# A recurrent chain's last step: the kept-back weight split is issued behind the copies of UV instead of behind the state update

## The chip, the cores and the metric

The kernel runs on one core of one Trainium2 chip. The metric is the device time of one execution in microseconds (us), lower is better; the time of a kernel is the median of several runs. Engines are named as in the profile: PE is TensorE's matmul, PEld its weight load, DVE is VectorE, ACT is ScalarE, POOL is GpSimd, and SP is the queue that issues nearly all DMAs.

## What is computed

One inference step of a hybrid streaming layer over 512 prompt positions and 64 sample positions (576 columns) with model width 2048: an RMSNorm, one input projection to 10880 columns, an RWKV-7 branch (16 heads of 64, a recurrent matrix state), a sliding-window attention branch, two output projections gated and merged, a last projection, the residual and a final norm. The part that matters here is the recurrence:

```
def step(S, inp):
    r_t, w_t, k_t, v_t, a_t, b_t = inp
    sa = jnp.einsum('bhij,bhj->bhi', S, a_t)
    S = S * w_t[:, :, None, :] + sa[..., None] * b_t[:, :, None, :] + v_t[..., None] * k_t[:, :, None, :]
    return S, jnp.einsum('bhij,bhj->bhi', S, r_t)

s_final, y = lax.scan(step, wkv0.astype(f32), seq)
```

The layer around it is `x + (sigmoid(m_a) * (y_a @ p_a) + sigmoid(m_b) * (y_b @ p_b)) @ w_o`. Everything is float32.

## The kernel before

**The dense products.** The 576 columns are held as two halves of 256 and 320 (PSUM tiles `ga` and `gb`). Every float32 weight and activation is split in a high and a low part, and a product is three matmuls. A `Job` is one block of 128 output rows. One *k-step* of it (`Job.step`) is six matmuls, L156 and L157 in turn, on one block of 128 inputs. Four k-steps use one *quarter* of the job's weights. A quarter is loaded by SP (L125, `wr`, three buffers) and split by `wsplit`: ACT copies it to `wh` (L131), DVE subtracts to get `wl` (L132). `prefetch` does this for up to four quarters ahead.

**The recurrence** is computed in chunks of 64 positions, for two heads at a time, in eight turns `p` = 0 to 7 of `rwkv`; half E of the partitions (0 to 63) holds one head, half O (64 to 127) the other. A turn first prepares three groups `g` of three chunks each: the tiles `T` (DVE, L578 and L579 for half E, then both again for half O), `BK` (POOL, L580 and L581), the products of both on PE (L586 for E, L587 for O), the transposes L600, their copy `TK` by ACT (L602), and the masked products `nm` and `T` by DVE (L590, L594). Between the groups PE runs k-steps, and the generator `before` does the norm of the previous turn (`tail`: products `s<-yhi,sums` at L186 and L187, then `yc`, `ysq`, `ysql`, ...). Then come the inverse of a triangular matrix (L619, L621, through DRAM to `XT`, L658 to L675) and the *chain*: seven steps of one chunk each and a last step with chunks 7 and 8 side by side. One step is

- the state update `SV` on DVE from the last step's PSUM (L692, L693), then PE L699;
- DVE copies the result to `r0` (L703, L704), then PE L708;
- DVE copies the result, negated, to `UV` (L711, L712), then PE L718 and L719 (the next state) and L724 and L727 (the outputs `py`);
- in the last step `so` (L730), the finished states, from the PSUM of L718 and L719, to DRAM; ACT copies `py` out (L738, L740) and POOL subtracts (L741, `ylo`).

PE's order is written by hand: one k-step of the current job stands between L699 and L708 (`c1`), one between L708 and L718 (`c2`), one behind L727 (`c3`). The orders of DVE, ACT, POOL and SP come from a scheduler that goes by data dependences and the order of the program. `issue_after(i)` adds only that what is traced in its block on i's engine is issued behind i.

**Work that is kept back.** Inside the chain (`holding` not empty) a `prefetch` that falls due after a quarter, and the `end` of a job (L227, L403, a DMA), go into the queue `held`. `flush(n)` takes up to n of them out. Before the change a step takes out one behind its state update, and one behind the copies of UV if more than two are held; what is left comes out at the chain's end. Line numbers below are those of the kernel before; in the changed kernel all lines from L697 on are one higher.

Of the kernel before, what the change touches and what calls it, by code (L numbers as in the profile page):

```python
# [45 lines left out]
def tile_layer(ctx: ExitStack, tc: tile.TileContext, A: dict):  # L46
# [34 lines left out]
    def pst():  # L81
        return ps.tile([P, 512], F32, tag="s", name="s")
# [12 lines left out]
    held, holding = deque(), []  # L95
# [7 lines left out]
    def flush(n=99):  # L103
        while held and n:
            held.popleft()()
            n -= 1
# [63 lines left out]
    def pump(n):  # L170
        for _ in range(n):
            if not jobs:
                return
            jobs[0].step()
# [390 lines left out]
    def rwkv(p, r, k, v, kk, Pd, Qd, b, gate, ahead, before):  # L565
# [114 lines left out]
        for cs in (*((c,) for c in range(7)), (7, 8)):  # L680
            g = cs[0] // 3
            T, NM, TK = Ts[g], NMs[g], TKs[g]
            at = [(n * L, c, c - 3 * g) for n, c in enumerate(cs)]
            w = len(cs) * L
            if cs[0] == 3 * g:
                py = pst()
            s0p = r2.tile([P, 2 * L], F32, tag="s0p", name="s0p")
            p0 = pst()
            for n, c, i in at:
                if c not in (0, 8):  # L690
                    sp, pt, prev = S_prev
                    dve.scalar_tensor_tensor(SV[E, c, 0:64], sp[E, 0:64], pt[E], prev[E, 0:64], op0=ALU.mult, op1=ALU.add)  # L692
                    tip.append(dve.scalar_tensor_tensor(SV[O, c, 64:128], sp[O, 0:64], pt[O], prev[O, 0:64], op0=ALU.mult, op1=ALU.add).ins)  # L693
                    with tc.issue_after(tip[-1]):
                        flush(1)
                pt = PT[:, c : c + 1]
                act(s0p[E, n : n + L], SV[E, c, 0:64], AF.Copy, scale=pt[E])  # L697
                act(s0p[O, n : n + L], SV[O, c, 64:128], AF.Copy, scale=pt[O])
                nc.tensor.matmul(p0[:, 2 * n : 2 * n + P], T[:, i, 0, :], SV[:, c, :], start=True, stop=True)  # L699
            r0 = r2.tile([P, 2 * L], F32, tag="r0", name="r0")  # L700
            p3 = p0[:, 0 : 2 * w].rearrange("p (i c) -> p i c", c=P)
            r3 = r0[:, 0:w].rearrange("p (i c) -> p i c", c=L)
            dve.tensor_copy(r3[E], p3[E, :, 0:64])  # L703
            with tc.issue_after(dve.tensor_copy(r3[O], p3[O, :, 64:128]).ins):  # L704
                pump(PUMP["c1"] + (cs[0] == 0) * PUMP["c0"])
            pu = pst()
            for n, c, i in at:
                nc.tensor.matmul(pu[:, n : n + L], XT[:, c, :], r0[:, n : n + L], start=True, stop=True)  # L708
            ui = slice(cs[0], cs[-1] + 1)
            pu3 = pu[:, 0:w].rearrange("p (i c) -> p i c", c=L)  # L710
            dve.tensor_scalar(UV[E, ui, 0:64], pu3[E], -1.0, None, op0=ALU.mult)  # L711
            tip.append(dve.tensor_scalar(UV[O, ui, 64:128], pu3[O], -1.0, None, op0=ALU.mult).ins)  # L712
            with tc.issue_after(tip[-1]):
                flush(1 if len(held) > 2 else 0)
                pump(PUMP["c2"])
            sp = pst()
            for n, c, i in at:
                nc.tensor.matmul(sp[E, n : n + L], TK[:, i, 0:64], UV[:, c, 0:64], start=True, stop=True)  # L718
                nc.tensor.matmul(sp[O, n : n + L], TK[:, i, 64:128], UV[:, c, 64:128], start=True, stop=True)  # L719
            S_prev = (sp, pt, s0p)  # L720
            for n, c, i in at:
                for u, h_ in ((0, E), (1, O)):
                    hc = slice(64 * u, 64 * u + 64)
                    nc.tensor.matmul(py[h_, i * 64 : (i + 1) * 64], SV[:, c, hc], T[:, i, 1, hc], start=True, stop=False)  # L724
                for u, h_ in ((0, E), (1, O)):
                    hc = slice(64 * u, 64 * u + 64)
                    nc.tensor.matmul(py[h_, i * 64 : (i + 1) * 64], UV[:, c, hc], NM[:, i, 128 + 64 * u : 192 + 64 * u], start=False, stop=True)  # L727
                if c >= 7:
                    so = r2.tile([P, L], F32, tag="so", name="so")
                    dve.scalar_tensor_tensor(so, sp[:, n : n + L], PT[:, c : c + 1], s0p[:, n : n + L], op0=ALU.mult, op1=ALU.add)  # L730
                    nc.sync.dma_start(A["wkv"][c - 7, p], so)
            pump(PUMP["c3"])
            if cs[-1] == 8:
                holding.pop()
                flush()
            if cs[-1] == 3 * g + 2:
                q = slice(g * 192, (g + 1) * 192)
                act(ysb[0][:, q], py[:, 0:192], AF.Copy)  # L738
                yr = r2.tile([P, 192], F32, tag="NU", name="yr", bufs=1)
                act(yr, py[:, 0:192], AF.Copy)  # L740
                pool.tensor_tensor(ysb[1][:, q], yr, ysb[0][:, q].bitcast(F32), op=ALU.subtract)  # L741
# [26 lines left out]
    tip = []  # L768
    for p in range(8):
        xs = shift_jobs(p + 1) if p < 7 else []  # L770
        gate = silu_job(M_GA + p, "gatea")
        if p == 0:
            r, k0, v = [need(j) for j in x0]
            cur = (r, v, *prepare(0, r, k0))
            pump(PUMP["first"])

        def ahead():
            if p == 7:
                return None
            r, k0, v = [need(j) for j in xs]  # L780
            return (r, v, *prepare(p + 1, r, k0))

        r, v, kk, Pd, Qd, k, b = cur
        cur, before = rwkv(p, r, k, v, kk, Pd, Qd, b, gate, ahead, before)
# [220 lines left out]
```

## Time and profile before

| | |
|---|---|
| median of 3 runs | 1768.52 us (1767.48 to 1769.36) |
| the profiled execution | 1767.89 us |
| its span, first to last instruction | 1766.1 us |
| mean granted clock of PE | 0.998 |
| chains, first to last | 485 us to 1302 us of the span |
| last steps of the chain, DVE L703 | 513.12, 633.50, 745.76, 857.78, 970.13, 1083.10, 1195.20, 1298.13 us |

Rows of the timeline read: start in us from the span's start, length in us, engine, line, operation, written tile <- read tiles, size, and in brackets how long the engine sat idle before it and what ended that. In a row that groups instructions, the figures behind the bar are busy us and mean ns of one, and behind the second bar the idle time before them and what ended it.

### The profile page before, as it was taken

What the parts mean: (1) busy time and instruction counts of PE and PEld (TensorE: products, weight loads), DVE (VectorE), ACT (ScalarE), POOL (GpSimd) and SP (SyncE); (2) the same over time, 40 slices, a digit from 0 to 9 for tenths busy, and PEclk for the clock granted to TensorE, in tenths of its full rate; (3) what the DMA queues carried; (4) which work ended last, traced back from release to release, by engine and by line L of the source; (5) the groups of instructions that cost most, each with busy time, mean ns of one, the idle gap of its engine ahead of it and who ended that gap; (6) DMA issues with size and microseconds to landing.
All of it is one profiled execution on the core that took longest, in us unless ns stands there. A gap on an engine that the chain in (4) does not pass through costs nothing.

```text
span 1766.1 us, 35853 instructions
## 1 busy us (share of the span) xinstructions
PE 1735.3 (98%) x14249; PEld 1693.5 (96%) x14249; DVE 1061.4 (60%) x2335; ACT 734.2 (42%) x1422; POOL 345.8 (20%) x448
## 2 busy tenths in 40 slices
PE   9999999999999999999999999999999999999997
PEld 8999999999989999999899998999999999999996
DVE  7445445466768577677776787867655444442223
ACT  7455545543343443444444444344244222243321
POOL 0112212342211422224122241231011000001111
PEclk9999999999999999999999999999999999999999
DMA  7322222233424233233232332333336443253323
GB/s 233 114 90 76 87 87 74 80 118 99 127 73 116 93 91 109 78 105 102 85 108 85 105 99 78 103 96 102 109 117 231 130 132 129 94 171 104 106 80 107
DMA packets 158343, 190.89 MB, mean 108 GB/s; under 512 B 52384, under 2 KB 81344, under 8 KB 158176
## 3 DMA queue, kind: packets, MB, share of 16 engines
q1 hardware_dynamic: 156896, 183.89, 33.2%
q0 software_dynamic: 1280, 4.72, 0.8%
q8 instruction: 112, 1.84, 0.4%
q14 instruction: 55, 0.45, 0.1%
HBM read 158.42 MB, written 27.03 MB: 105 GB/s over the span
## 4 chain that ended last, share of the span: by engine, by line
PE 82%; DVE 10%; issue 3%; DMA 3%; ACT 1%; POOL 1%; SPq 0%; DVEq 0%; ACTq 0%; POOLq 0%
PE gb L157 38%; PE ga L156 31%; DVE wl L132 2%; DVE XU L621 1%; DVE tmp L619 1%; PE s L708 1%; PE s L718 1%; DMA XT<-x_d 1%; PE s L699 1%; PE s L157 1%; PE s L187 1%; DVE T L578 1%; DVE T L579 1%; PE s L324 1%; DMA yraw<-ya_d 1%
## 5 line engine op out<-in xcount | busy, mean ns | idle before, releaser
L131 ACT ACTIVATE wh<-wr 128x512 fp32r<-128x512 f32 x460 | 287.1, 628 | 576.6 <-PE gb L157 488.3
L132 DVE TENSOR_TENSOR wl<-wr,wh 128x512 fp32r<-128x512 f32 x460 | 329.1, 720 | 232.3 <-ACT wh L131 228.3
L860 POOL TENSOR_TENSOR sq<-sq 128x256 f32<-128x256 f32 (+1 forms) x28 | 24.9, 905 | 371.3 <-ACT sq L854 371.3
L619 DVE TENSOR_TENSOR tmp<-NU,XU 108x84 f32<-108x84 f32 (+23 forms) x248 | 65.4, 264 | 23.2 <-DMA NU<-n_d 14.8
L621 DVE TENSOR_TENSOR XU<-XU,tmp 108x84 f32<-108x84 f32 (+23 forms) x248 | 69.4, 280 | 6.4
L741 POOL TENSOR_TENSOR ylo<-yr,yhi 128x192 fp32r<-128x192 f32 x24 | 18.0, 751 | 271.3 <-ACT yr L740 237.2
L697 ACT ACTIVATE s0p<-SV,PT 64x64 f32<-64x64 f32 x72 | 25.0, 347 | 70.7 <-DVE SV L692 57.6
L238 POOL COPY praw<-praw 128x7 f32<-128x7 f32 x25 | 9.2, 369 | 212.2 <-DVE praw L235 212.1
L348 ACT ACTIVATE sc<-sc,nm 128x256 f32<-128x256 f32 (+2 forms) x80 | 37.1, 466 | 13.6 <-DVE nm L346 13.5
L403 ACT ACTIVATE sg<-sg 128x576 f32<-128x576 f32 x32 | 21.9, 684 | 46.7 <-DVE sg L227 46.1
L254 POOL TENSOR_TENSOR gateb<-gateb,z 128x576 f32<-128x576 f32 x8 | 11.4, 1422 | 150.3 <-ACT gateb L253 150.3
L581 POOL TENSOR_TENSOR BK<-k,Qd 64x192 f32<-64x192 f32 x48 | 33.3, 695 | 35.2 <-DVE k L560 34.6
L353 POOL TENSOR_TENSOR sc<-sc,es 128x768 f32<-128x768 f32 x16 | 27.6, 1725 | 63.7 <-ACT wh L131 58.0
L711 DVE TENSOR_SCALAR UV<-s 64x64 f32<-64x64 f32 x64 | 14.4, 225 | 41.3 <-PE s L708 41.1
L692 DVE SCALAR_TENSOR_TENSOR SV<-s,PT,s0p 64x64 f32<-64x64 f32 x56 | 15.5, 276 | 38.4 <-PE s L719 33.1
L580 POOL TENSOR_TENSOR BK<-b,Qd 64x192 f32<-64x192 f32 x48 | 33.4, 696 | 11.8 <-PE s L600 8.9
L708 PE MATMUL s<-r,XT 128*128 128x64 f32 x144 | 27.2, 279 | 7.4 <-DVE r L704 7.4
L241 POOL TENSOR_TENSOR d<-praw 128x576 f32<-128x576 f32 x25 | 34.4, 1375 | 0.0
L708 PEld LDWEIGHTS s<-r,XT 128*128 128x128 f32 x144 | 21.1, 188 | 12.2 <-issue 6.9
L756 DVE RECIPROCAL sd<-sd 128x576 f32<-128x576 f32 x8 | 29.9, 3741 | 2.7 <-ACT sd L755 2.7
L242 DVE SCALAR_TENSOR_TENSOR d<-d,vec,praw 128x576 f32<-128x576 f32 x25 | 21.9, 875 | 14.7 <-POOL d L241 14.7
L556 DVE RECIPROCAL nrm<-nrm 128x576 f32<-128x576 f32 x8 | 30.0, 3751 | 1.1 <-ACT nrm L555 1.1
(1147 smaller groups left out, 7216.4 us busy)
## 6 DMA issues: line engine op xcount, KB each, us to landing
wr<-in_w_in SPq DMA_DIRECT2D x340, 256.0 KB
wr<-in_w_o SPq DMA_DIRECT2D x56, 256.0 KB
sg_d<-sg SPq DMA_DIRECT2D x32, 288.0 KB
sg<-sg_d SPq DMA_DIRECT2D x32, 288.0 KB
wr<-in_p_b SPq DMA_DIRECT2D x32, 256.0 KB
wr<-in_p_a SPq DMA_DIRECT2D x32, 256.0 KB
x<-in_xT SPq DMA_DIRECT2D x16, 288.0 KB
n_d<-nm SPq DMA_DIRECT2D x24, 192.0 KB
```

Of the source, the lines that this page charges most:

```text
L131: act(hi, src, AF.Copy)
L132: dve.tensor_tensor(lo, src, hi.bitcast(F32), op=ALU.subtract)
L156: nc.tensor.matmul(self.pa[:, :NA], w[:, k % QK, :], x[:, 0:NA], start=f, stop=e)
L157: nc.tensor.matmul(self.pb[:, :NB], w[:, k % QK, :], x[:, NA:NT], start=f, stop=e)
L241: pool.tensor_tensor(d, p[:, :, 0:64], p[:, :, 1:65], op=ALU.subtract)
L348: act(sc[:, a:b], sc[:, a:b], AF.Exp, bias=nm[:, i : i + 1], accum_out=dn[:, i : i + 1])
L556: dve.reciprocal(nrm, nrm)
L580: pool.tensor_tensor(BK[h_, :, 64 * u : 64 * u + 64], b[h_, cs_, :], Qd[h_, cs_, :], op=ALU.mult)
L581: pool.tensor_tensor(BK[h_, :, 64 - 64 * u : 128 - 64 * u], k[h_, cs_, :], Qd[h_, cs_, :], op=ALU.mult)
L619: dve.tensor_tensor(t_, NU[:, j, j + 1 : UB].unsqueeze(1).to_broadcast([SP * UN, m, n]), XU[:, 0:m, j : j + 1].to_broadcast([SP * UN, m, n ...
L621: dve.tensor_tensor(XU[:, 0:m, j + 1 : UB], XU[:, 0:m, j + 1 : UB], t_, op=ALU.add)
L708: nc.tensor.matmul(pu[:, n : n + L], XT[:, c, :], r0[:, n : n + L], start=True, stop=True)
```

## The change

In the last step of each of the eight chains nothing is taken out of `held` behind the state update any more, and up to two things are taken out behind the copies of UV. The other seven steps stay as they are.

```
@@ -691,8 +691,9 @@
                     sp, pt, prev = S_prev
                     dve.scalar_tensor_tensor(SV[E, c, 0:64], sp[E, 0:64], pt[E], prev[E, 0:64], op0=ALU.mult, op1=ALU.add)
                     tip.append(dve.scalar_tensor_tensor(SV[O, c, 64:128], sp[O, 0:64], pt[O], prev[O, 0:64], op0=ALU.mult, op1=ALU.add).ins)
-                    with tc.issue_after(tip[-1]):
-                        flush(1)
+                    if c < 7:
+                        with tc.issue_after(tip[-1]):
+                            flush(1)
                 pt = PT[:, c : c + 1]
...
             tip.append(dve.tensor_scalar(UV[O, ui, 64:128], pu3[O], -1.0, None, op0=ALU.mult).ins)
             with tc.issue_after(tip[-1]):
-                flush(1 if len(held) > 2 else 0)
+                flush(2 if cs[0] == 7 else 1 if len(held) > 2 else 0)
                 pump(PUMP["c2"])
```

PE's and POOL's orders are the same in both kernels. DVE's differs from each last step on. First the last step of the chain at p = 1 (the same at p = 2 to 6), from the state update to the first T tiles of the next turn; before:

```order
L692 SCALAR_TENSOR_TENSOR SV<-s,PT,s0p 64x64
L693 SCALAR_TENSOR_TENSOR SV<-s,PT,s0p 64x64
L132 TENSOR_TENSOR wl<-wr,wh 128x512
L703 COPY r_7879<-s 64x128
L704 COPY r_7879<-s 64x128
L711 TENSOR_SCALAR UV<-s 64x2x64
L712 TENSOR_SCALAR UV<-s 64x2x64
L578 TENSOR_TENSOR T<-kk,Pd 64x3x64
L579 TENSOR_TENSOR T<-d,Pd 64x3x64
L578 TENSOR_TENSOR T<-kk,Pd 64x3x64
L730 SCALAR_TENSOR_TENSOR so<-s,PT,s0p 128x64 x2
L579 TENSOR_TENSOR T<-d,Pd 64x3x64
```

The same place on DVE in the changed kernel:

```order
L692 SCALAR_TENSOR_TENSOR SV<-s,PT,s0p 64x64
L693 SCALAR_TENSOR_TENSOR SV<-s,PT,s0p 64x64
L704 COPY r_7873<-s 64x128
L705 COPY r_7873<-s 64x128
L712 TENSOR_SCALAR UV<-s 64x2x64
L713 TENSOR_SCALAR UV<-s 64x2x64
L132 TENSOR_TENSOR wl<-wr,wh 128x512
L731 SCALAR_TENSOR_TENSOR so<-s,PT,s0p 128x64 x2
L578 TENSOR_TENSOR T<-kk,Pd 64x3x64
L579 TENSOR_TENSOR T<-d,Pd 64x3x64
L578 TENSOR_TENSOR T<-kk,Pd 64x3x64
L579 TENSOR_TENSOR T<-d,Pd 64x3x64
```

The split stands behind the copies of UV, and it and both `so` now stand ahead of all four T instructions of group 0.

The second place is further on at p = 1 on DVE: the masked products of group 0, the next split, the end of a job (`sg`), and T of group 2; before:

```order
L579 TENSOR_TENSOR T<-d,Pd 64x3x64
L590 TENSOR_TENSOR nm_4328<-s,con 64x6x64
L594 TENSOR_TENSOR T<-s,con 64x6x64
L590 TENSOR_TENSOR nm_4328<-s,con 64x6x64
L594 TENSOR_TENSOR T<-s,con 64x6x64
L132 TENSOR_TENSOR wl<-wr,wh 128x512
L227 TENSOR_TENSOR sg<-rstd,ga 128x256
L227 TENSOR_TENSOR sg<-rstd,gb 128x320
```

In the changed kernel:

```order
L590 TENSOR_TENSOR nm_4328<-s,con 64x6x64
L594 TENSOR_TENSOR T<-s,con 64x6x64
L590 TENSOR_TENSOR nm_4328<-s,con 64x6x64
L132 TENSOR_TENSOR wl<-wr,wh 128x512
L594 TENSOR_TENSOR T<-s,con 64x6x64
L227 TENSOR_TENSOR sg<-rstd,ga 128x256
L227 TENSOR_TENSOR sg<-rstd,gb 128x320
L579 TENSOR_TENSOR T<-d,Pd 64x3x64
```

One L579 of T's group 2 has moved from ahead of these rows to behind the two L227, the split has moved ahead of the last L594, and the last L579 of group 2 (not shown) stands behind the masked products of group 1.

The third place is the last step at p = 0 on DVE, where the end of a job is held beside the split; before:

```order
L132 TENSOR_TENSOR wl<-wr,wh 128x512
L227 TENSOR_TENSOR sg<-rstd,gb 128x320
L703 COPY r_6317<-s 64x128
L704 COPY r_6317<-s 64x128
L711 TENSOR_SCALAR UV<-s 64x2x64
L712 TENSOR_SCALAR UV<-s 64x2x64
L578 TENSOR_TENSOR T<-kk,Pd 64x3x64
L579 TENSOR_TENSOR T<-d,Pd 64x3x64
L578 TENSOR_TENSOR T<-kk,Pd 64x3x64
L730 SCALAR_TENSOR_TENSOR so<-s,PT,s0p 128x64 x2
L579 TENSOR_TENSOR T<-d,Pd 64x3x64
```

In the changed kernel:

```order
L704 COPY r_6311<-s 64x128
L705 COPY r_6311<-s 64x128
L712 TENSOR_SCALAR UV<-s 64x2x64
L713 TENSOR_SCALAR UV<-s 64x2x64
L132 TENSOR_TENSOR wl<-wr,wh 128x512
L227 TENSOR_TENSOR sg<-rstd,ga 128x256
L227 TENSOR_TENSOR sg<-rstd,gb 128x320
L731 SCALAR_TENSOR_TENSOR so<-s,PT,s0p 128x64 x2
L578 TENSOR_TENSOR T<-kk,Pd 64x3x64
L579 TENSOR_TENSOR T<-d,Pd 64x3x64
L578 TENSOR_TENSOR T<-kk,Pd 64x3x64
L579 TENSOR_TENSOR T<-d,Pd 64x3x64
```

Here both L227 as well stand ahead of T (the first of them stood ahead of the state update before); behind these rows come the next split, half E of T's group 1, the four masked products of group 0, and only then half O of group 1. At p = 7, which has no next turn, two splits, both L227 and both `so` follow the copies of UV, and on ACT the end of the job (L403) has moved from ahead of the last step's copies `s0p` to between the copies of `py` (L738, L740) and those of the norm (L748).

More of the change, by code (lines that the diff above doesn't have):

```diff
@@ L693, in rwkv @@
                     tip.append(dve.scalar_tensor_tensor(SV[O, c, 64:128], sp[O, 0:64], pt[O], prev[O, 0:64], op0=ALU.mult, op1=ALU.add).ins)
-                    with tc.issue_after(tip[-1]):
-                        flush(1)
+                    if c < 7:
+                        with tc.issue_after(tip[-1]):
+                            flush(1)
                 pt = PT[:, c : c + 1]
@@ L713, in rwkv @@
             with tc.issue_after(tip[-1]):
-                flush(1 if len(held) > 2 else 0)
+                flush(2 if cs[0] == 7 else 1 if len(held) > 2 else 0)
                 pump(PUMP["c2"])
```

## Prediction

> **What bounds the kernel now.** First the page: PE is busy nearly the whole span, and the chain that ended last is mostly PE.
>
> ```profile
> PE 1735.3 (98%) x14249; PEld 1693.5 (96%) x14249; DVE 1061.4 (60%) x2335; ACT 734.2 (42%) x1422; POOL 345.8 (20%) x448
> PE 82%; DVE 10%; issue 3%; DMA 3%; ACT 1%; POOL 1%; SPq 0%; DVEq 0%; ACTq 0%; POOLq 0%
> ```
>
> So only PE's own gaps can be won or lost; DVE at 60% matters where PE waits for it. Second, the groups of PE rows by form between 480 and 1302 us: three waits recur.
>
> ```profile
> L708 PE MATMUL s<-r,XT 128*128 128x64 f32 x144 | 27.2, 279 | 7.4 <-DVE r L704 7.4
> L187 PE MATMUL s<-yhi,sums 128*128 128x320 f32 x7 | 2.9, 414 | 4.7 <-ACT TK L602 4.7
> L673 PE MATMUL s<-XT,Y 32*32 32x32 f32 x288 | 7.2, 193 | 1.8 <-DVE Y L668 1.6
> ```
>
> PE waits 7.4 us for `r0` (L704), 4.7 us for `TK`, 1.8 us for `Y`. Third, the timeline of the last step at p = 1; the offsets at p = 2 to 6 are the same within 0.03 us.
>
> ```profile
> 631.37 0.29 DVE L693 SCALAR_TENSOR_TENSOR SV<-s,PT,s0p 64x64 f32<-64x64 f32 x1
> 631.98 0.60 PE L699 MATMUL s<-SV,T 128*128 128x128 f32 x4
> 632.11 0.63 ACT L131 ACTIVATE wh<-wr 128x512 fp32r<-128x512 f32 x1
> 632.78 0.69 DVE L132 TENSOR_TENSOR wl<-wr,wh 128x512 fp32r<-128x512 f32 x1 [1.12 <-ACT wh L131]
> 633.50 0.28 DVE L703 COPY r<-s 64x128 f32<-64x128 f32 x1
> 633.80 0.29 DVE L704 COPY r<-s 64x128 f32<-64x128 f32 x1
> 634.24 0.63 PE L708 MATMUL s<-r,XT 128*128 128x64 f32 x4 [0.86 <-DVE r L704]
> ```
>
> DVE stands 1.12 us idle because the split waits for `wh`, then works 0.69 us on it, and only then copies `r0`, which PE needs. L699 to L708 takes 2.26 us.
>
> **Term 1: the wait at L708.** At p = 7 the split is out of the way: `wh` came early, and DVE was through with the split before PE's product was (the bracket behind L703).
>
> ```profile
> 1297.49 0.61 PE L699 MATMUL s<-SV,T 128*128 128x128 f32 x4
> 1298.13 0.28 DVE L703 COPY r<-s 64x128 f32<-64x128 f32 x1 [0.24 <-PE s L699]
> 1298.87 0.63 PE L708 MATMUL s<-r,XT 128*128 128x64 f32 x4
> 512.28 0.60 PE L699 MATMUL s<-SV,T 128*128 128x128 f32 x4
> 513.85 0.63 PE L708 MATMUL s<-r,XT 128*128 128x64 f32 x4 [0.17 <-DVE r L704]
> ```
>
> L699 to L708 is 1.38 us there. So p = 1 to 6 win 2.26 - 1.38 = **0.88 us each**; p = 0 (last two rows, 1.57 us) wins 0.19; p = 7 nothing. Sum 5.47 us.
>
> **Term 2: what is late next.** The split does not vanish; it now stands ahead of T, and PE's L586 and L587 of the next turn wait for T.
>
> ```profile
> 635.22 0.30 DVE L712 TENSOR_SCALAR UV<-s 64x128 f32<-64x128 f32 x1
> 635.88 0.22 PE L719 MATMUL s<-UV,TK 128*64 128x64 f32 x1
> 636.58 0.48 DVE L730 SCALAR_TENSOR_TENSOR so<-s,PT,s0p 128x64 f32<-128x64 f32 x2
> 637.09 0.35 DVE L579 TENSOR_TENSOR T<-d,Pd 64x192 f32<-64x192 f32 x1
> 637.24 0.66 POOL L741 TENSOR_TENSOR ylo<-yr,yhi 128x192 fp32r<-128x192 f32 x1 [8.03 <-ACT yr L740]
> 637.48 0.63 DVE L578 TENSOR_TENSOR T<-kk,Pd 64x192 f32<-64x192 f32 x1
> 637.59 0.34 PE L587 MATMUL s<-T,BK 64*128 64x128 f32 x1
> 638.42 0.55 PE L600 MATMUL s<-con,BK 128*128 128x128 f32 x3
> ```
>
> Call u the end of the copies of UV (635.52 here). T of half O ends at 637.44, and L587 starts 0.15 us behind it: T has no slack today. After, from u: split 0.03 to 0.72; both `so` 0.75 to 1.23 (PE's L719 starts at u + 0.36, so they hardly wait); T of half E to 1.87. POOL's `ylo` starts at u + 1.72 as now. Beside it the T row of 637.48 took 0.63 us against 0.35; I charge the first L578 of half O the same, so half O ends at about u + 2.8, L587 starts at 2.96 (now 2.07) and L600, 0.83 us behind it, at about 3.8 (now 2.90). PE waits **some 0.9 us more**, all of term 1.
>
> The Trainium skill, page "SBUF — State Buffer", section "Who interferes with whom", says that a Vector instruction with two SBUF inputs contends with a GpSimd one that reads SBUF. By that rule T beside `ylo` is held, and the 0.63 us agrees; were T not held, the sum below would be 1.6 us better.
>
> **Term 3: the wait that takes this up.** Further on PE waits at L187.
>
> ```profile
> 639.05 0.59 POOL L580 TENSOR_TENSOR BK<-b,Qd 64x192 f32<-64x192 f32 x1 [1.16 <-PE s L600]
> 643.50 0.47 DVE L227 TENSOR_TENSOR sg<-rstd,gb 128x320 f32<-128x320 f32 x1
> 644.00 0.68 ACT L403 ACTIVATE sg<-sg 128x576 f32<-128x576 f32 x1 [3.81 <-DVE sg L227]
> 644.17 0.28 PE L186 MATMUL s<-yhi,sums 128*128 128x256 f32 x1
> 644.59 0.47 ACT L602 ACTIVATE TK<-s 128x384 f32<-128x384 f32 x1
> 645.12 0.41 PE L187 MATMUL s<-yhi,sums 128*128 128x320 f32 x1 [0.67 <-ACT TK L602]
> ```
>
> L187 could follow L186 by 0.12 us; it starts 0.83 us late, because `TK` stands on ACT behind L403, and that waits for DVE's L227, which ends at u + 8.45. PE 0.9 us later reaches L187 at 9.60 - 0.83 + 0.9 = u + 9.7. Does L227 stay early enough? It must end by u + 8.55, since L187 came 1.15 us behind it. DVE's work ahead of L227 grows by the split (0.72) and shrinks by one L579, which has moved behind it (0.35 us or more). POOL's four instructions start behind L600, so now 0.9 us later; then they meet the second split and the masked products, which read PSUM, rather than T. I get L227's end at about u + 8.35, just early enough. So L187 starts at u + 9.7 against 9.60 now: of term 2 **only 0.1 us is left** per turn. p = 1 to 6 keep 6 x (0.88 - 0.1) = 4.7 us.
>
> **p = 0** has both L227 ahead of T as well; the first two rows are groups over all turns, the others its own.
>
> ```profile
> L590 DVE TENSOR_TENSOR nm<-s,con 64x384 f32<-64x384 f32 x42 | 23.1, 549 | 0.1
> L227 DVE TENSOR_TENSOR sg<-rstd,ga 128x256 f32<-128x256 f32 x26 | 10.7, 412 | 2.6 <-PE ga L156 2.3
> 514.83 0.29 DVE L712 TENSOR_SCALAR UV<-s 64x128 f32<-64x128 f32 x1
> 518.04 0.55 PE L600 MATMUL s<-con,BK 128*128 128x128 f32 x3
> 520.91 0.37 PE L586 MATMUL s<-T,BK 64*128 64x128 f32 x1
> 524.73 0.41 PE L187 MATMUL s<-yhi,sums 128*128 128x320 f32 x1 [0.67 <-ACT TK L602]
> ```
>
> From u = 515.12: the split, the two L227 (0.41 and 0.47 us), both `so`, then T of half O ends at about 3.5; L587 comes at 3.7, L600 at 4.5 (now 2.92). Half O of group 1 stands behind the four masked products (2.2 us at 0.549), which wait for L587: it ends near u + 7.9, and PE, 2.87 us from L600 to the next L586, would want it at 7.4; with 0.15 us to PE 0.6 us more are lost. L187, now at u + 9.61 with 0.83 us of wait, comes at 9.61 - 0.83 + 1.6 + 0.6 = 11.0. With the 0.19 won: **1.2 us lost** (0.6 to 2.0).
>
> **p = 7.** L403 now stands ahead of the norm's copies on ACT and ends about u + 3.1, behind split, L227, split, L227 and its own 0.68 us; u is 1300.15, 1.28 us behind L708 as at p = 1.
>
> ```profile
> 1302.60 0.38 ACT L748 ACTIVATE yc<-s 128x256 f32<-128x256 f32 x1 [0.80 <-PE s L186]
> 1305.54 0.38 PE L186 MATMUL s<-ysql,sums 128*128 128x256 f32 x1
> ```
>
> `yc` slips by 0.6 us, and PE's L186 of `ysql`, only some 0.1 us behind its turn today, by the same: **0.6 us lost** (0 to 0.7).
>
> **L673.** On ACT the norm's copies of a turn stand behind this `s0p` of the next turn's first step, which waits for a memset; in the changed order they stand ahead of it.
>
> ```profile
> 646.99 0.35 ACT L697 ACTIVATE s0p<-SV,PT 64x64 f32<-64x64 f32 x1 [1.41 <-DVE SV L649]
> ```
>
> So `ysql` and all that DVE has behind it, down to `tail`'s reciprocal, come some 0.5 us earlier (an estimate from that 1.41 us and a memset that comes 1.1 us later), and from there one line of work leads to `Y`. The waits there at p = 2, 4, 5, 6 (in all 1.8 us) shrink: **1.0 us won** (0 to 1.6).
>
> **At nothing:** the split is done 1.9 us later, and SP's next load of `wr`, which waits for it, too. PE still reads the quarter before it beyond L600 at 638.42, 3 us behind the new end at 635.4; `ready` holds up to four. Were that cover gone, each turn would cost up to 1.9 us. The later `so` feed only a store.
>
> **Sum:** 4.7 - 1.2 - 0.6 + 1.0 = 3.9 us. The profiled execution, 1767.89 us (1.79 us outside its span), becomes 1764.0. It lies 0.63 us under the median of 1768.52, to which the forecast refers: **1764.6 us**.
>
> **The rivals.** *A, nothing is held:* the first L578 of half O escapes POOL, L587 comes 0.27 us earlier and the slack at L187 covers the rest: 6 x 0.27 better, 1763.0 us. For it: POOL might come second. Against: the 0.63 us stands in all turns. Chance 0.15.
>
> *B, L227 slips:* the second split, now ahead of the last L594 and beside POOL, is held, and L227 ends near u + 9.0; L187 comes at 10.15, 0.45 us worse than forecast at six turns: 1764.6 + 2.7 = 1767.3 us. For it: by my count L227 has only 0.2 us to spare. Chance 0.27.
>
> *C, slower:* L227 ends at u + 9.35 or later, so that L187 takes all of term 1 again (9.35 + 1.15 - 9.60 = 0.90), and L673 gains nothing: 1768.52 + 1.2 + 0.6 + 0.1 = 1770.4 us; a further 0.3 us at six turns would give 1772.2. It decides from an end of L227 about 0.9 us behind today's 8.45. Against: the moved work is 0.72 us less one T instruction. Chance 0.10.
>
> *D, it does not do what it says:* PE keeps waiting at L708, because DVE waits for L699 anyway, and T is late all the same: 1768.5 + 0.6 + 1.4 + 0.6 - 1.0 = 1770.1 us. Against: the p = 7 rows. Chance 0.03. The forecast keeps 0.45.
>
> **Range and chances.** Ends of the bounds: all good 1761, all bad 1772. 8 in 10 lie between 1762.3 and 1769.0. About 0.2% (3.5 us) is what a measurement of this kernel can tell from no change, and the forecast lies 3.9 us under the median, just beyond it. Six tenths of the forecast case and nearly all of A lie under 1765.0, about a tenth of B: faster 0.44. Slower by 3.5 us needs C at its worst: 0.04. The same: 0.52.
>
> **What would show it.** Right: no wait at L708 in the last steps at p = 0 to 6; L699 to L708 about 1.4 us; L587 near u + 3.0 at p = 1 to 6 and the wait at L187 gone; a new wait at p = 0 before both first L587 groups. Wrong: L227 ending behind u + 8.6 (then B or C), L587 near u + 2.7 (then A), or a wait of PE for a `wl` of the moved split.

## The result and the profile after

The changed kernel takes 1759.7 us (median of 6 runs, 1759.3 to 1761.34), beside it before 1768.94 us (6 runs, 1767.48 to 1771.72): ratio 0.9948, 95% interval 0.9937 to 0.9958. That is 9.2 us faster where 3.9 us were forecast, and below the range. The span went from 1766.1 to 1757.9 us. Over all sessions the kernel before took between 1767.5 and 1773.0 us, and its profiled execution, 1767.89 us, lies near the fast end, so what an edit wins is read below from stretches of the traces and not from the times alone. The changed kernel's page, busy time of the engines and chain of waits:

```profile
PE 1734.1 (99%) x14249; PEld 1694.2 (96%) x14249; DVE 1063.0 (60%) x2335; ACT 737.3 (42%) x1422; POOL 341.4 (19%) x448
PE 94%; DVE 3%; issue 1%; DMA 1%; ACT 0%; POOL 0%; SPq 0%; DVEq 0%; ACTq 0%; POOLq 0%
```

PE is busy as long as before in a shorter span, and DVE's share of the chain fell from 10% to 3%. PE's waits in the changed kernel, and one row of PEld's waits in the kernel before (us in total, times, longest):

```profile
PE s L587 <- DVE T L579: 3.3, 8, 0.5
PE s L709 <- DVE r L705: 2.1, 3, 0.7
PE s L186 <- DVE ysql L91: 0.3, 1, 0.3
PEld s L673 <- DVE Y L668: 3.4, 10, 0.9
```

The waits at L187 for `TK` and at L673 for `Y` have no row any more; a new one for T stands at L587. The last row is the one that the prediction did not read: by weight loads, L673 of the kernel before waits 3.4 us, not 1.8. The timeline of the last step at p = 1 in the changed kernel:

```profile
633.28 0.38 PE L700 MATMUL s<-SV,T 128*128 128x128 f32 x2
633.92 0.28 DVE L704 COPY r<-s 64x128 f32<-64x128 f32 x1 [0.96 <-PE s L700]
634.65 0.29 PE L709 MATMUL s<-r,XT 128*128 128x64 f32 x1
635.64 0.29 DVE L713 TENSOR_SCALAR UV<-s 64x128 f32<-64x128 f32 x1
635.96 0.69 DVE L132 TENSOR_TENSOR wl<-wr,wh 128x512 fp32r<-128x512 f32 x1
636.69 0.48 DVE L731 SCALAR_TENSOR_TENSOR so<-s,PT,s0p 128x64 f32<-128x64 f32 x2
637.72 0.75 DVE L578 TENSOR_TENSOR T<-kk,Pd 64x192 f32<-64x192 f32 x1
638.89 0.34 PE L587 MATMUL s<-T,BK 64*128 64x128 f32 x1 [0.49 <-DVE T L579]
643.58 0.47 DVE L227 TENSOR_TENSOR sg<-rstd,gb 128x320 f32<-128x320 f32 x1
645.59 0.31 PE L187 MATMUL s<-yhi,sums 128*128 128x320 f32 x1
645.73 0.28 PE L186 MATMUL s<-ylo,sums 128*128 128x256 f32 x1
```

L700 to L709 is 1.37 us. With u = 635.93, L587 comes at u + 2.96, L227 ends at u + 8.12, L187 comes at u + 9.66 without a wait. All of this is within 0.25 us of the forecast; the gain that was missed is elsewhere.

To find it, the program from L699 of the last step at p = 0 to L699 at p = 7 is cut in five stretches, read from the timelines of PE and DVE and summed over the turns. `ylo` stands for the first matmul with `ylo`, the mark at the norm's first product, and `ysql` for the first one with `ysql` in its second product. The first mark comes 0.26 us behind an L187 that waited (9.86 us behind UV in the kernel before, where L187 is at 9.60). The expectations of the last experiments count to it too.

| stretch, us | before | after | won |
|---|---|---|---|
| L699 to L708, p = 0 to 6 | 15.13 | 9.66 | 5.47 |
| L708 to the end of UV, same | 8.94 | 8.90 | 0.04 |
| end of UV to `ylo`, p = 0 | 9.86 | 11.09 | -1.23 |
| the same, p = 1 to 6 | 59.12 | 58.81 | 0.31 |
| `ylo` to `ysql` on PE | 35.84 | 35.57 | 0.27 |
| `ysql` to L699 of the next last step | 656.32 | 652.54 | **3.78** |
| all | 785.21 | 776.57 | 8.64 |

The last stretch holds L673. Why it shrank shows on ACT and DVE at p = 1, first one row of the kernel before, where `s0p` is at 646.99, then the changed kernel:

```profile
647.25 0.36 ACT L748 ACTIVATE yc<-s 128x256 f32<-128x256 f32 x1
646.05 0.39 ACT L749 ACTIVATE yc<-s 128x256 f32<-128x256 f32 x1
648.13 0.35 ACT L698 ACTIVATE s0p<-SV,PT 64x64 f32<-64x64 f32 x1 [0.77 <-DVE SV L649]
653.39 3.75 DVE L757 RECIPROCAL sd<-sd 128x576 f32<-128x576 f32 x1
```

The norm's copies stood behind `s0p` and now stand ahead of it. The reciprocal comes at u + 17.46; before it came at 653.78, u + 18.26. The line of work behind it, first in the kernel before, then in the changed one (POOL, DVE, SP's queue, DVE):

```profile
653.78 3.74 DVE L756 RECIPROCAL sd<-sd 128x576 f32<-128x576 f32 x1
657.60 2.69 POOL L757 TENSOR_TENSOR yc<-yc,sd 128x576 f32<-128x576 f32 x1 [1.41 <-DVE sd L756]
658.32 0.68 DVE L132 TENSOR_TENSOR wl<-wr,wh 128x512 fp32r<-128x512 f32 x1
663.53 0.33 SPq L762 DMA_DIRECT2D ya_d<-yc  x1
663.91 0.40 SPq L613 DMA_DIRECT2D NU<-n_d  x1
667.90 0.19 DVE L619 TENSOR_TENSOR tmp<-NU,XU 108x31 f32<-108x31 f32 x1 [2.86 <-DMA NU<-n_d]
```

```profile
657.23 1.76 POOL L758 TENSOR_TENSOR yc<-yc,sd 128x576 f32<-128x576 f32 x1 [1.57 <-DVE sd L757]
658.07 1.46 DVE L132 TENSOR_TENSOR wl<-wr,wh 128x512 fp32r<-128x512 f32 x1
662.21 0.33 SPq L763 DMA_DIRECT2D ya_d<-yc  x1
662.59 0.40 SPq L613 DMA_DIRECT2D NU<-n_d  x1
666.55 0.19 DVE L619 TENSOR_TENSOR tmp<-NU,XU 108x31 f32<-108x31 f32 x1 [1.34 <-DMA NU<-n_d]
```

SP issues the last load of `NU` only behind the store of `yc`, and the substitution (L619, L621), XT and `Y` wait for that load. The store comes 1.73 us earlier behind UV (28.01 to 26.28): 0.80 us from the reciprocal, 0.93 because POOL's product takes 1.76 us, not 2.69, beside the same split.

### The profile page after: what moved, and what is told of

Its sections match the earlier page's. It is cut to its first block, busy times and chain, and to the rows that moved or that the text cites. A ratio compares the mean times of both kernels' runs of the same rounds, so it can differ in the third digit from the quotient of the medians.

```text
span 1757.9 us, 35846 instructions
## 1 busy us (share of the span) xinstructions
PE 1734.1 (99%) x14249; PEld 1694.2 (96%) x14249; DVE 1063.0 (60%) x2335; ACT 737.3 (42%) x1422; POOL 341.4 (19%) x448
## 4 chain that ended last, share of the span: by engine, by line
PE 94%; DVE 3%; issue 1%; DMA 1%; ACT 0%; POOL 0%; SPq 0%; DVEq 0%; ACTq 0%; POOLq 0%
PE gb L157 44%; PE ga L156 36%; PE s L709 1%; PE s L700 1%; PE s L719 1%; PE s L586 1%; PE s L157 1%; PE s L187 1%; PE s L324 1%; PE s L600 1%; PE s L156 1%; DVE wl L132 1%; DMA yraw<-ya_d 1%; PE s L186 1%; PE s L323 1%
## 5 line engine op out<-in xcount | busy, mean ns | idle before, releaser
L132 DVE TENSOR_TENSOR wl<-wr,wh 128x512 fp32r<-128x512 f32 x460 | 334.8, 731 | 238.8 <-ACT wh L131 234.3
L619 DVE TENSOR_TENSOR tmp<-NU,XU 108x84 f32<-108x84 f32 (+23 forms) x248 | 65.3, 263 | 14.1 <-DMA NU<-n_d 8.5
L621 DVE TENSOR_TENSOR XU<-XU,tmp 108x84 f32<-108x84 f32 (+23 forms) x248 | 69.3, 280 | 6.4
L403 ACT ACTIVATE sg<-sg 128x576 f32<-128x576 f32 x32 | 21.9, 685 | 37.2 <-DVE sg L227 36.5
L704 DVE COPY r<-s 64x64 f32<-64x64 f32 x64 | 14.4, 225 | 25.3 <-PE s L700 23.9
L709 PE MATMUL s<-r,XT 128*128 128x64 f32 x144 | 27.2, 279 | 2.1 <-DVE r L705 2.1
```

The source lines that it names most:

```text
L132: dve.tensor_tensor(lo, src, hi.bitcast(F32), op=ALU.subtract)
L619: dve.tensor_tensor(t_, NU[:, j, j + 1 : UB].unsqueeze(1).to_broadcast([SP * UN, m, n]), XU[:, 0:m, j : j + 1].to_broadcast([SP * UN, m, n ...
L621: dve.tensor_tensor(XU[:, 0:m, j + 1 : UB], XU[:, 0:m, j + 1 : UB], t_, op=ALU.add)
```

## The experiments

The theory: what was forecast as 1.0 us at L673 is about 4 us, and ACT's order alone makes it. The rival: it comes from the split's new place. A turn is named below by the last step that it follows, so "behind p = 4" is the stretch up to the last step at p = 5.

**Only ACT's order.** The kernel before; the last entry of `norm` is the copy `ysqh` (L90), and the lines that fill the list are left out here. DVE's and PE's orders are unchanged.

```
-                act(s0p[E, n : n + L], SV[E, c, 0:64], AF.Copy, scale=pt[E])
-                act(s0p[O, n : n + L], SV[O, c, 64:128], AF.Copy, scale=pt[O])
+                with tc.issue_after(norm[-1]) if norm and c == 0 else nullcontext():
+                    act(s0p[E, n : n + L], SV[E, c, 0:64], AF.Copy, scale=pt[E])
+                    act(s0p[O, n : n + L], SV[O, c, 64:128], AF.Copy, scale=pt[O])
```

> The kernel before, with one thing changed: from the second turn on, ScalarE does the first chain step's two s0p behind the norm copies of the turn ahead (yc, ysq, yc, ysq, ysqh, then s0p) and not ahead of them. The split stays behind the state update, so the waits at L708 (2.26 us from L699 to L708) and at L187 (9.6 us behind the copies of UV) stay. Theory: what the forecast sized at 1.0 us (the waits at L673, with the start of the norm's product ahead of it) comes from this order: the norm copies stood behind s0p, which wait for the clearing of SV, and reciprocal and inverse copies on VectorE came that much late. It expects L673 to wait no more in six turns, 2 us there and 1.5 to 2 us ahead of it, 1 us at the product of the norm, together 4 to 5 us: 1764 to 1765 us where before has 1768.9, and the reciprocal some 0.7 us earlier behind the product's start. Rival: the gain at L673 in the changed kernel comes from where the split now stands (TensorE arrives elsewhere), and the order on ScalarE alone does nothing: within 0.5 us of before, the waits at L673 as before.

Measured 1763.19 us against 1771.28 beside it, ratio 0.9958 (0.9943 to 0.9972). From the first to the last L699: 780.81 us, 4.40 less. The waits of PE (lines shifted by up to 3; L711 is L708, L189 is L187):

```profile
PE s L711 <- DVE r L707: 7.4, 10, 0.9
PE s L189 <- ACT TK L604: 4.0, 6, 0.7
```

L708 and L187 wait as before (in one turn less at L187, since p = 0 has lost its wait there, 0.93 us), and neither PE nor PEld has a row for L673 left. The last stretch is 653.04 us, 3.3 less, `ylo` to `ysql` 35.62, 0.2 less, and the reciprocal comes 2.58 us behind its product, not 3.29. The theory holds for 3.5 of its 4 us. Most of the 0.5 us that is missing lies in two turns, behind p = 2 and 4, where a load is slow (the load of `XT`, below).

**The split behind the copies of r0.** The changed kernel, but the split fills the 0.81 us in which DVE waits for L708. DVE's order is then T of half E, `so`, T of half O; on ACT `s0p` stands ahead of the norm's copies again.

```
             with tc.issue_after(dve.tensor_copy(r3[O], p3[O, :, 64:128]).ins):
+                flush(cs[0] == 7)
                 pump(PUMP["c1"] + (cs[0] == 0) * PUMP["c0"])
...
-                flush(2 if cs[0] == 7 else 1 if len(held) > 2 else 0)
+                flush(1 if len(held) > 2 else 0)
```

> The changed kernel, but the split of the last chain step stands between the two copies of r0 and the two of UV, where VectorE waits 0.81 us for TensorE's L708 in the kernel before, and takes 0.69 us itself. Order on VectorE: state update, copies of r0, split, copies of UV, two of T, so, the others of T. All theories: L699 to L708 is 1.38 us as in the changed kernel. Term 2 as forecast (the split and so ahead of T make T late): L587 is back at some 2.1 us behind the copies of UV and not 2.96. Theory on L187 (VectorE's and ScalarE's work ahead of TK sets it, whatever T does): 9.6 us behind UV in turns 1 to 6, so nothing won there; 1.3 us won in the first turn. Theory on L673 (it is ScalarE's order that removes the wait, and here s0p stands ahead of the norm copies again): the waits there come back, 4 to 5 us, and the whole is 1762 to 1763.5 us. Rival (the place of the split removes the wait at L673): the gain there stays, and the whole is 1 to 2 us below the changed kernel, 1758 us.

1766.36 us, ratio 0.9973 (0.9963 to 0.9982). PE's waits:

```profile
PE s L187 <- ACT TK L602: 5.4, 7, 0.8
PE s L673 <- DVE Y L668: 4.8, 8, 1.3
```

L699 to L708 is 1.38 us, L587 comes 1.99 us behind UV, and `ylo` still at 9.91 in turns 1 to 6: T on time wins nothing while L187 waits for TK. That is terms 2 and 3 of the prediction. The waits at L673 are back, larger than expected: the last stretch is 663.30 us, 7 more than before. Two turns (behind p = 4 and 5) lost some 3 us each against the changed kernel: 1.2 and 1.5 us are PE's waits at L673, and right behind them the granted clock was 0.57 from 1054 to 1058 us and from 1166.5 to 1170.5 us, where the other turns have 1.00 (4 us at 0.57 are 1.7 us of work not done, an estimate). Why it fell there is not shown; behind p = 1 PE waited 1.4 us and it stayed at 1.00. So a split that is no longer behind the state update does not remove the waits by itself.

**Both edits together:**

> The kernel with the split behind the copies of r0, with ScalarE's first s0p of a turn behind the norm copies as well (both edits run apart before). L699 to L708 1.38 us, L587 2.0 us behind the copies of UV, no wait at L673, reciprocal 2.6 us behind its product. Theory: L187 waits for TK behind L403 behind L227 again, at 9.9 us, so that T on time wins nothing in turns 1 to 6; the first turn wins 1.2 us over the changed kernel or more. Span 1 us below the changed kernel's, 1757 us. Rival: T on time is worth its 0.9 us a turn, 1751 us.

1757.47 us, ratio 0.9931 (0.9916 to 0.9946); `ylo` at 9.91 us in turns 1 to 6, 8.86 at p = 0; the last stretch 652.66, as in the changed kernel. The theory holds; of the waits that the prediction counts, L189 (L187) for TK is left:

```profile
PE s L189 <- ACT TK L604: 4.7, 6, 0.8
```

**Turns 1 to 6 only:**

```
-                    if c < 7:
+                    if c < 7 or p in (0, 7):
...
-                flush(2 if cs[0] == 7 else 1 if len(held) > 2 else 0)
+                flush(2 if cs[0] == 7 and 0 < p < 7 else 1 if len(held) > 2 else 0)
```

> The changed kernel, but in the first turn and the last the split stays behind the state update; turns 1 to 6 are as changed. Theory: the first turn loses by the change (T of the next turn late by 1.3 us, against 0.2 us won at L708), since nothing waits at its L187 that could take the delay; the last gains 0.3 us. So this kernel is 0.8 us faster than the changed one in the span of the trace, with L187 of the second turn 9.6 us behind the copies of UV again, where the changed kernel has 10.9. Rival: the first turn's delay is taken up further on (at L673 of the second turn, which waits no more), and the span is within 0.3 us of the changed kernel's.

1758.93 us, span 1757.0. At p = 0 `ylo` is back at 9.85 us (1.24 us won) and L699 to L708 at 1.57 (0.19 lost); 0.6 us of waiting at L673, behind p = 4, hides part of it. At p = 7, L703 to `ysql` is 7.41 us as in the kernel before. The first turn's loss is as forecast, and nothing takes it up.

**T beside POOL's `ylo`.** POOL's subtraction for the low part of y is left out in the third group of p = 0 to 6; ACT copies y there.

```
+                if g == 2 and p < 7:
+                    act(ysb[1][:, q], yr, AF.Copy)
+                else:
+                    pool.tensor_tensor(ysb[1][:, q], yr, ysb[0][:, q].bitcast(F32), op=ALU.subtract)
```

> The changed kernel, but GpSimd's subtraction for the low part of y is left out in the third group of turns 0 to 6, where it runs beside T; a copy on ScalarE stands in its place, so the low part holds the whole of y there. Theory (a product on VectorE with two inputs from SBUF is held by GpSimd's subtraction): the third row of T, 0.75 us in the changed kernel, takes 0.35 us, L587 comes 0.4 us earlier, some 2.6 us behind the copies of UV, L600 with it; L187 stays at 9.65 us, since it is not T that sets it but TK behind L227, so the span of turns 1 to 6 stays within 0.3 us, and the first turn, where nothing takes the delay up, gains up to 0.4 us. Rival (T is late for another reason, and L187 follows T): the row stays at 0.75 us, or L187 comes 0.3 us earlier in every turn, 2 us in all.

1758.0 us in a single run. The same T row, and L587, with u at 634.65:

```profile
636.44 0.35 DVE L578 TENSOR_TENSOR T<-kk,Pd 64x192 f32<-64x192 f32 x1
637.22 0.34 PE L587 MATMUL s<-T,BK 64*128 64x128 f32 x1
```

0.35 us against 0.75, and L587 at 2.57 us, 0.39 earlier. But `ylo` came 0.39 us earlier too, 9.41 us behind UV in turns 1 to 6 (10.77 at p = 0): the expectation was wrong there and its rival right. In the changed kernel T sets L187, not TK; the stretch from UV to `ylo` in turns 1 to 6 went from 58.81 to 56.45 us. Waits at L673, 2 us of them behind p = 4, hid most of that.

**TK ahead of the gate's sigmoid,** in the kernel before and in the changed one. If T sets L187 now, taking TK out from behind L403 helps only before. DVE's and PE's orders stay.

```
-            act(s, s, AF.Sigmoid)
+            def gate():
+                act(s, s, AF.Sigmoid)
...
+            late.append(gate) if tk else gate()
...
+            i = act(TK, s[:, 0:384].rearrange("p (i c) -> p i c", i=3), AF.Copy)
+            if g == 1:
+                tk.pop()
+                with tc.issue_after(i.ins):
+                    while late:
+                        late.pop(0)()
```

> The kernel before, but on ScalarE the sigmoid of the gate (L403) stands behind the second group's TK and not ahead of it; the orders of the other engines are as before. Theory (the wait at L187 is TK standing behind L403, which waits for the scaling at L227): L187 comes 8.9 us behind the copies of UV and not 9.86, in all seven turns, 6 us in the span together, if nothing behind it takes that up; the waits at L708 and L673 stay. Rival (TK itself is late, by its transposes or its bank): L187 stays at 9.86 us.

> The changed kernel with the same reordering on ScalarE: the gate's sigmoid behind the second group's TK. Theory (in the changed kernel the late T has taken the wait at L187 up, so L187 follows L587 and no longer TK): nothing, L187 stays at 9.80 us behind the copies of UV in turns 1 to 6 and at 11.1 in the first. Rival (TK still sets it): 8.9 to 9.4 us, 3 to 5 us in the span.

In the kernel before, `ylo` came at 8.92 us in turns 1 to 6 (at p = 0 it stayed at 9.86), 5.6 us won. PE's waits say where they went:

```profile
PE s L685 <- DVE Y L680: 3.7, 8, 1.2
PE s L187 <- ACT ysqh L90: 1.4, 6, 0.2
```

L685 is L673 and L187 is L186: the second row is the norm's second product, which waits for `ysqh`, late behind `s0p` on ACT. `ylo` to `ysql` grew from 35.84 to 41.44 us, which takes all 5.6 back, and the last stretch by 4 us more, 2.7 of them behind p = 1, where PE waited 1.4 us at L673 and the granted clock was 0.50 from 720 to 722 us: 1771.4 us in a single run, against 1769.36. In the kernel before, a wait removed ahead of `s0p` is only moved.

In the changed kernel `ylo` stayed at 9.80 and 11.11 us, as the theory had it. Its single run, 1761.78 us, is longer by 2.4 us in the last stretch, nearly all of it waiting at L673 behind p = 1 and 4, though DVE and PE have the same orders as in the changed kernel. What differs is SP's load of `XT` (L658, here L670), for which DVE's transposes `Xe` (L660, here L672) wait. Behind p = 4, first in the changed kernel, then in this one:

```profile
1031.00 0.39 SPq L658 DMA_DIRECT2D XT<-x_d  x1
1035.71 0.95 DVE L660 STREAM_TRANSPOSE Xe<-XT 32x288 f32<-32x288 f32 x2 [1.85 <-DMA XT<-x_d]
```

```profile
1030.89 0.39 SPq L670 DMA_DIRECT2D XT<-x_d  x1
1037.36 0.95 DVE L672 STREAM_TRANSPOSE Xe<-XT 32x288 f32<-32x288 f32 x2 [3.64 <-DMA XT<-x_d]
```

Both issue the load 63.2 to 63.3 us behind UV; from there to `Xe` it is 4.71 us and 6.47 us. Behind p = 1 to 6 of the changed kernel's trace it is 4.48 to 4.71 us, and L673 does not wait. The waits above that came back behind p = 4 go with the same: 5.63 us with the change in turns 1 to 6 only, 6.90 us with the low part on ACT. Why this load takes longer in some turns is open.

**All three edits:**

> As the one ahead of it, and ScalarE does the second group's TK ahead of the gate's sigmoid. Theory: with T on time (2.0 us behind the copies of UV) and TK free of L403, L187 comes 8.9 us behind them in every turn, 0.9 us earlier than in the changed kernel in turns 1 to 6 and 2.2 us in the first: span 1750 to 1751 us, time 1752 to 1753 us. Rival (what is won at L187 is lost at the next waiting place, at L673 or at the products' banks): within 2 us of the changed kernel.

1750.69 us (4 runs, 1750.07 to 1751.43), ratio to before 0.9894 (0.9877 to 0.991), **some 9 us faster than the changed kernel**. `ylo` comes at 8.86 us in all turns. Of PE's waits of over 1 us in all these are left:

```profile
PE s L725 <- DVE r L720: 2.1, 3, 0.7
PE ga L159 <- ACT wh L134: 1.4, 2, 0.8
PE s L217 <- DVE heat L214: 1.4, 1, 1.4
```

**The line from the reciprocal to `Y`,** in two kernels, each the kernel before with one edit: the product of `yc` on DVE, and the store of `yc` issued by POOL and not by SP.

```
-            pool.tensor_tensor(yc, yc, sd, op=ALU.mult)
+            dve.tensor_tensor(yc, yc, sd, op=ALU.mult)
```

> The kernel before, with one instruction moved from GpSimd to VectorE: the product of yc with the reciprocal (L757), which takes 2.69 us on GpSimd beside the splits in the kernel before and 1.76 us in the changed one. ScalarE's and TensorE's orders around it stay. Theory (what is late at L673 is one line: reciprocal, yc on GpSimd, ScalarE, GpSimd again, VectorE, the store of yc on SP, and the third load of NU that SP issues behind that store, the substitution, XT, Y): the store comes about 2 us earlier behind the copies of UV, and the waits at L673 go although ScalarE's order, the start of the reciprocal (3.3 us behind the product of ysql), L708 and L187 are as before; 3 to 4 us in the span of turns 1 to 6. Rival (Y is late by something else that ScalarE's order sets, the clearing of SV or the masked products behind ysql): the waits at L673 stay within 1 us of the 3.7 us of before.

```
-            nc.sync.dma_start(ya_d[p], flat(yc))
+            nc.gpsimd.dma_start(ya_d[p], flat(yc))
```

> The kernel before, with the store of yc (L762) issued by GpSimd and not by SP; the norm itself is as late as before. Theory (SP issues the third load of NU behind that store, and the substitution starts with that load): the substitution starts 2 us or more earlier behind the copies of UV, and the waits at L673 go in turns 1 to 6, 3 to 4 us; the reciprocal stays 3.3 us behind its product and the wait of VectorE for yc too. Rival (the substitution starts late because VectorE itself stands at yc): it starts as late as before, and L673 keeps its waits.

The first: 1764.84 us, ratio 0.9968 (0.9956 to 0.998); the store came 26.45 us behind UV (661.75 less 635.30), not 28.01, and the last stretch fell by 1.9 us; the waits behind p = 2 and 4 stayed, where the load of `XT` took 5.26 and 5.87 us. The second: 1764.19 us, ratio 0.9965 (0.9952 to 0.9977); the last stretch fell by 3.0 us, and no wait at L673 is left, while the reciprocal stays 3.29 us behind its product. SP's load of `NU` and two of PE's waits there:

```profile
658.61 0.39 SPq L613 DMA_DIRECT2D NU<-n_d  x1
PE s L708 <- DVE r L704: 7.4, 10, 0.9
PE s L187 <- ACT TK L602: 4.7, 7, 0.7
```

With u at 634.70 the load goes out at u + 23.9, not 28.4. Nor does `Xe` wait for the load of `XT` any more: DVE is idle for at most 0.12 us ahead of it behind p = 1 to 5, where it was 1.6 to 1.9 us in the changed kernel. So the waits at L673 come from a load that stands behind a store on SP, with the time of the load of `XT` on top. Making the store earlier by 1.6 or 1.7 us, as the product on DVE and the changed kernel do, was enough where that load took under 5 us, and not where it took 5.6 us or more.

## Why the prediction was wrong

**Right, by size too.** *Term 1:* 5.47 us forecast, 5.47 measured. *Term 2:* L587 at u + 2.96, as forecast; POOL's `ylo` holds T (0.75 us against 0.35 without it). *Term 3:* the wait at L187 takes the delay up; forecast 0.1 us left per turn, measured 0.05 us won to `ylo`, since the matmul that follows a wait also takes longer (0.41 us against 0.31 at L187). L227 ended at u + 8.12 where 8.35 was forecast, so rivals B and C did not come; A did not since T is held. *p = 0:* 1.2 us lost forecast, 1.23 less the 0.19 won measured; L187 at 11.0 forecast, 10.94 measured.

**p = 7** was charged at twice what it cost: from r0's copy (L703) to PE's L186 of `ysql` 7.41 us before (1298.13 to 1305.54), 7.72 after: 0.31 us lost, not 0.6.

**The step that failed is the term L673.** Its mechanism was right: the norm's copies leave their place behind `s0p`, and one line of work leads from there to `Y`. Its size was not: 1.0 us, at most 1.6, against 3.78 in the last stretch and 0.27 ahead of `ysql`. Three things made the difference:

- The bound. The prediction took PE's idle time ahead of L673 (1.8 us) as all that could be lost there. That figure counts from the modelled ends of the matmuls ahead, and PEld's row has 3.4 us. With the store off SP, 3.0 us of the last stretch went and `ysql`'s part stayed.
- `ysql` itself. Its product stood late behind `s0p` in turns 1 to 6, about 0.05 us ahead of it and 0.12 behind it each (what the last stretch still has over 652.54 us in the kernel with the store off SP, 0.74 us, by six; there its two matmuls, L186 and L187, start 0.23 us apart, in the changed kernel 0.12): some 1.0 us, counted as nothing.
- The earliness. 0.5 us was forecast for the reciprocal, 0.80 came, and POOL's product added 0.93. So every one of these waits went in the profiled execution, where the forecast had them shrink by half. That no load of `XT` was slow in it is luck; slow ones brought 0.6 to 2.4 us of them back in other traces.

With 3.0 + 1.0 in place of 1.0 at L673, 0.3 in place of -0.6 for the rest of turns 1 to 6 and -0.3 at p = 7, the sum becomes 5.5 + 0.3 - 1.2 - 0.3 + 4.0 = 8.3 us; the spans differ by 8.2.

## What to carry to other kernels

Bound a wait of PE by the longest of what the profile offers: PE's bracket, PEld's wait, and the difference of the same stretch between turns that wait and turns that don't. Where ScalarE stands in order behind a copy that waits for a late clearing, look at all that it delays, down to the DMA queues: a load behind a store is as late as the store's data. An edit that removes a wait pays only where nothing late comes next; here the same edit to TK won nothing in the kernel before and in the changed one (a single run each, both some 2 us longer), and 7 us in a third. And a single trace shows only the waits of that execution: a load that is usually done in time can be late in the next.

## What the hardware showed

The same two instructions, POOL's product of `yc` and a split on DVE, shared the time in two ways: 2.69 and 0.68 us in the kernel before, 1.76 and 1.46 in the changed one; POOL's figures stand so in all of turns 1 to 6. The split began 0.72 us behind POOL's start in the first and 0.84 us in the second; another split had begun 0.15 us ahead of POOL in both. With all three edits the later split began 0.71 us behind POOL and took 1.59 us, POOL's product 1.76 us, so the distance alone does not settle it. The Trainium skill, page "SBUF — State Buffer", section "Who interferes with whom", says that issue order decides which of two contending engines blocks. In all three POOL's row starts ahead of the later split, and yet the loser differs; what decides it here stays open.
